# Loads placed behind the cast that frees their buffer, and every small transfer of attention and norms put on the sync queue

## The chip, the cores and the metric

The kernel runs on one core of a Trainium2 chip. A core has five engines that each work through their own list of instructions in order: PE (matrix products), DVE (vector), ACT (scalar), POOL (GpSimd) and SP (the sync engine, which here only issues DMA transfers). [...] The metric is the device time of one execution in microseconds (us), the median of several runs.

## The reference

A trunk of two layers on 256 tokens of width 2048, in float32. Each layer is a token mixer and an MLP, both behind an RMS norm and added into one residual stream:

```
for i in range(DEPTH):                                   # DEPTH = 2
    h = rms_norm(x, mix_norm_g[i])
    mix = fox_attention(...) if i % 2 == 0 else dilated_attention(...)
    x = x + mix
    h = rms_norm(x, mlp_norm_g[i])
    x = x + sq_relu_mlp(h, mlp_w_up[i], mlp_w_down[i])   # (relu(h @ up) ** 2) @ down
```

- `fox_attention`: 16 heads of 128. `h @ w_in` gives q, k, v and a forget gate per head; q and k are RMS-normed per head with a gain; the scores get the difference of cumulated log-sigmoid gates as a bias; causal softmax; `@ w_out`.
- `dilated_attention`: 8 heads with three groups of q and k each (dilations 1, 4, 16) and a shared v of 256; each group is a causal window of 128 strided steps with an ALiBi slope; the three groups are merged by their softmax denominators, which is one softmax over all of them; `@ w_out`.
- The MLP goes from 2048 to 8192 and back.

## The kernel before

**Weights.** All weights, some 420 MB, stream through the core once. `plan` (L207 to L257) lists pieces of 256 rows by 512 columns (512 KB), 800 of them, in the order of their use. `load()` (L280) puts one piece into one of five raw buffers (`RAW_BUFS`) by a transfer on the sync queue; in the dilated layer, where the columns of q and k lie apart, by two transfers of 256 KB. `split()` (L297) makes a high part `wh` in a reduced float format on ACT (L309, "the cast") and the rest `wl` by a subtraction on DVE (L310, "the cut"), each in five buffers (`W_BUFS`). A product is then three matmuls (L340 to L342): high by high, low by high, high by low; the MLP's first product (`transposed_steps`, L392) puts them into two (L404, L408). The matmuls of these weight products are called the main matmuls below. A raw buffer is free once cast and cut of its piece are done, and a pair of `wh` and `wl` once PE is through with its piece. `product_steps` (L330) calls `split()` after each piece, and `split()` calls `load()` first if its piece has not been asked for.

The fox layer's heads go in four groups of four: a weight product for q, one for k, one for v, and the heads' own work beside the next products.

**Side work.** Attention and norms run as Python generators under `Jobs` (L43). A `yield 4` means: go on four steps of the running weight product later; a step is one slice of 128 rows. `behind(x)` makes what is issued inside it stand behind the instruction `x` in its engine's list. Within these rules a planner in the framework, which works with its own estimates of durations, decides the final order of every engine's list when the program is built. The lists are fixed from then on; semaphores make an instruction wait for its inputs.

**Transposes through DRAM.** Several small matrices are transposed in 32 by 32 blocks on DVE, and the blocks are put into their places by writing them to DRAM and reading them back:

- `transposed_by_dma` (L431), for the norms: per token half four block writes (L440) and a read (L442), all on the sync queue, one behind the other.
- `qk_chain` (L513), for the heads' q and k: per token half four block writes on the sync queue (L544) and a read on POOL's queue (L545); the results are used 12 steps later.
- `p_turned` (L600), for softmax probabilities: four block writes (L610) one step after the transposition, and four steps later the read (L614), all on ACT's queue.

Also, `fox_head` (L730) loads each head's row of gate sums, spread over all partitions, on ACT's queue (`bias`, L742), and `gate_chain` writes them to DRAM on the sync queue (L727). `p_split` (L618) casts the turned probabilities (L623, L625) and `pv` (L584) multiplies them with v on PE (L593, L594, tiles `po_f` and `po_d`). `scores` (L653) computes a head's scores (tiles `sc_f`, `sc_d`; L657, L660); in the dilated layer DVE adds the ALiBi table (L799, tile `sd`). The last heads of a layer are transposed on PE instead (`p_transposed`, L628).

**The start.** Five pieces and x are loaded first; `more_constants` (L160) then loads the gate's weights `wf` (L164) and the gains, behind the load issued last at that point; `gate` (L667) multiplies with them (tile `pf`).

Of the kernel before, what the change touches and what calls it, by code (L numbers as in the profile page):

```python
# [89 lines left out]
def trunk(ctx: ExitStack, tc, x, fox_w_in, fox_b_f, fox_q_gain, fox_k_gain, fox_w_out, dil_w_in,  # L90
# [169 lines left out]
    def behind(*instructions):  # L260
        stack = ExitStack()
        for i in instructions:
            stack.enter_context(tc.issue_after(getattr(i, "ins", i)))
        return stack

    def hold(first):

        if "held" not in issued:
            return ExitStack()
        with behind(issued["gained"]):  # L270
            nc.vector.memset(first, 0.0)
        return behind(*([issued["load"]] if issued["held"] == [] else []))
# [24 lines left out]
    def split():  # L297
        i = state["split"]
        per = RAW_SUB // W_SUB
        if i >= len(plan) * per:  # L300
            return
        if i % per == 0 and state["raw"] <= i // per:
            load()
        raw = raws[i // per][:, (i % per) * W_SUB:(i % per + 1) * W_SUB, :]
        hi = wpool.tile([P, W_SUB, NC], F32R, tag="wh", name=f"wh{i}", bufs=W_BUFS)
        lo = wpool.tile([P, W_SUB, NC], F32R, tag="wl", name=f"wl{i}", bufs=W_BUFS)
        with behind(*([issued["gained"]] if i == 0 else issued.get("n0", []) if i < 2 * W_BUFS else [])):
            for part in ([slice(0, 1), slice(1, 2)] if i < 1 else [slice(0, W_SUB)]):
                issued["cast"] = nc.scalar.copy(hi[:, part, :], raw[:, part, :])  # L309
                issued["cut"] = nc.vector.tensor_sub(lo[:, part, :], raw[:, part, :], hi[:, part, :].bitcast(F32))  # L310
        splits.append((hi, lo))
        state["split"] += 1

# [114 lines left out]
    def transposed_by_dma(tag, col, n):  # L430


        tiles = []
        for t in range(NT):
            tile_ = work.tile([P, NC], F32, tag="w", name=f"turned_{tag}_{n}_{t}", bufs=5)
            blocks = dram.tile([4, 32, 4, P], F32, tag="blocks", name=f"blocks_{tag}_{n}_{t}", bufs=4)
            nc.vector.transpose(tile_.rearrange("p (j b r) -> p b j r", j=4, b=4),
                                xt[n][:, t, :].rearrange("p (b j c) -> p b j c", j=4, c=32))
            for i in range(4):
                nc.sync.dma_start(blocks[:, :, i, :].rearrange("j c x -> c j x"),  # L440
                                  tile_[32 * i:32 * i + 32].rearrange("p (j x) -> p j x", j=4))
            nc.sync.dma_start(tile_, blocks.rearrange("j c i x -> (j c) (i x)"))  # L442
            tiles.append(tile_)
        yield 9
        for half in range(2):
            pr = n * 2 + half
            both = act.tile([P, 2, 2, S], F32R, tag="hT", name=f"hT_{tag}_{pr}", bufs=KC // 2)
            for i in range(2):
                gc = gain[:, col + pr * 2 + i:col + pr * 2 + i + 1]
                for t in range(NT):  # L450
                    src = tiles[t].rearrange("p (i b r) -> p b i r", i=4, b=4)[:, half * 2 + i]
                    hi, lo = (both[:, i, x, t * P:(t + 1) * P].rearrange("p (i r) -> p i r", i=4) for x in range(2))
                    with behind(issued["cast"]):
                        on_act = nc.scalar.activation(hi, src, AF.Copy, scale=gc)
                    with behind(issued["cut"]):
                        on_dve = nc.vector.scalar_tensor_tensor(lo, src, gc, hi.bitcast(F32), ALU.mult, ALU.subtract)
            issued[tag, pr] = issued[tag] = on_act, on_dve
            hT[tag][pr] = both
            jobs.done.add((tag, pr))
            yield 1  # L460
# [52 lines left out]
    def qk_chain(acc, tag, key, parts):  # L513
# [21 lines left out]
            qn.append(q)  # L535


        for t in range(NT):
            turned = sq[t].rearrange("p (j h r) -> p j h r", j=4, h=4)
            nc.vector.transpose(turned.rearrange("p j h r -> p h j r"),  # L540
                                qn[t].rearrange("p h (j c) -> p h j c", c=32))
            blocks = dram.tile([4, 32, 4, P], F32, tag="blocks", name=f"blocks_{key}_{t}", bufs=4)
            for i in range(4):
                nc.sync.dma_start(blocks[:, :, i, :].rearrange("j c x -> c j x"), sq[t][32 * i:32 * i + 32].rearrange("p (j x) -> p j x", j=4))  # L544
            nc.gpsimd.dma_start(qn[t], blocks.rearrange("j c i x -> (j c) (i x)").rearrange("p (h d) -> p h d", h=4))  # L545
        yield 12
        for t in range(NT):
            yield 2
            for n, (c, nh, gcol, (whole, hi, lo)) in enumerate(parts):
# [50 lines left out]
    def p_turned(p, name):  # L600


        turned = work.tile([P, 4, 3, 32], F32, tag="s", name=f"turned_{name}", bufs=S_BUFS)
        nc.vector.transpose(turned.rearrange("p j b r -> p b j r"), p.rearrange("p (b j c) -> p b j c", b=3, c=32))
        yield 1

        blocks = dram.tile([4, 32, 4, 3 * 32], F32, tag="pblocks", name=f"pblocks_{name}", bufs=4)
        for i in range(4):
            with behind(issued["cast"]):
                nc.scalar.dma_start(blocks[:, :, i, :].rearrange("j c x -> c j x"),  # L610
                                    turned[32 * i:32 * i + 32].rearrange("p j b r -> p j (b r)"))
        yield 4
        with behind(issued["cast"]):
            nc.scalar.dma_start(turned.rearrange("p i b r -> p (i b r)"), blocks.rearrange("j c i x -> (j c) (i x)"))  # L614
        yield 4
        return turned

    def p_split(turned, name):  # L618
# [55 lines left out]
    def gate_chain(tag, pf):  # L674
# [49 lines left out]
        ct = work.tile([FH, 3 * P], F32, tag="s", name="g_ct", bufs=S_BUFS)  # L724
        nc.vector.tensor_scalar(ct[:, P:], pct, -1.0, None, ALU.mult)
        nc.vector.tensor_copy(ct[:, 0:P], ct[:, P:2 * P])
        nc.sync.dma_start(negc, ct)  # L727
        jobs.done.add("gate")

    def fox_head(j, hh, qT, kT, vt):  # L730
# [7 lines left out]
            yield at - 4  # L738

        bias = work.tile([P, 3 * P], F32, tag="bias", name=f"bias{h}", bufs=2)  # L740
        with behind(issued["cast"]):
            nc.scalar.dma_start(bias, negc[h:h + 1, :].to_broadcast([P, 3 * P]))  # L742
        yield 4
        nc.vector.tensor_add(bias, bias, tables["mask"])
        if hh == 0:
# [40 lines left out]
    def dil_head(q4, i, qTs, kTs, vt):  # L786
        h = 2 * q4 + i
        for g in range(3):
            yield ("dqk", q4, g)
        yield (3 if q4 == 3 else 6) * i + 1  # L790
        s = work.tile([P, 3, 3 * P], F32, tag="sd", name=f"sd{h}", bufs=1)
        for g in range(3):
            yield ("table", g)
            ps = ps_sc.tile([P, 512], F32, tag="sc", name=f"sc_d{h}_{g}")
            with behind(issued["product"]):
                for t in range(NT):
                    scores(ps, t, qTs[g], kTs[g], i)
            slope = 2.0 ** (-8.0 * (g * DH + h + 1) / N_SLOPES)
            nc.vector.scalar_tensor_tensor(s[:, g, :], tables[g], -slope, ps[:, 0:3 * P], ALU.mult, ALU.add)  # L799
            yield 1  # L800
        nm = small.tile([P, NT], F32, tag="nm", name=f"nm_d{h}")
        den = small.tile([P, NT], F32, tag="den", name=f"den_d{h}")
        spans = [slice(0, P), slice(P, 3 * P)]
        for t in range(NT):
            nc.vector.tensor_reduce(nm[:, t:t + 1], s[:, :, spans[t]], AX.XY, ALU.max, negate=True)
        yield 1
        for t in range(NT):
            nc.scalar.activation(s[:, :, spans[t]], s[:, :, spans[t]], AF.Exp, bias=nm[:, t:t + 1],
                                 accum_out=den[:, t:t + 1])
        yield 1  # L810
        nc.vector.reciprocal(den, den)
        p = work.tile([P, 3 * P], F32, tag="s", name=f"p_d{h}", bufs=S_BUFS)
        nc.vector.tensor_add(p, s[:, 0, :], s[:, 1, :])
        nc.vector.tensor_add(p, p, s[:, 2, :])
        for t in range(NT):
            nc.vector.tensor_scalar_mul(p[:, spans[t]], p[:, spans[t]], den[:, t:t + 1])
        if (q4, i) == (3, 1):
            yield 2
            pt_sb = p_transposed(p, f"d{h}")
        else:  # L820
            turned = yield from p_turned(p, f"d{h}")
            yield ("dv", q4)
            pt_sb = p_split(turned, f"d{h}")
        yield 3
        hi, lo = (act.tile([P, 2, S], F32R, tag=f"aT{x}", name=f"oTd{x}_{h}", bufs=KC // 2) for x in "hl")
        oT["d", h] = hi, lo
        yield from pv(pt_sb, vt, [i * S, i * S + P], [hi[:, 0, :], hi[:, 1, :]], [lo[:, 0, :], lo[:, 1, :]], f"d{h}")
        jobs.done.add(("od", h))
# [206 lines left out]
```

## Time and profile before

| | us |
|---|---|
| median of 3 runs (2158.12 to 2165.82) | 2159.53 |
| the profiled execution's own time | 2161.2 |
| its span, first to last instruction | 2159.5 |

| engine | busy us | share of the span |
|---|---|---|
| PE | 2142.0 | 99% |
| DVE | 1411.1 | 65% |
| ACT | 1098.5 | 51% |
| POOL | 66.0 | 3% |

The mean granted clock of PE is 0.998 of full speed. The sync queue carries 446 MB in transfers that take 65.9% of the 16 DMA engines' time, ACT's queue 12 MB (2.1%), POOL's 10.5 MB (1.5%). The fox layer's attention ends at about 330 us, the first MLP at about 1050, the dilated attention at about 1430, and the second MLP ends the run.

In the rows of the profile, `L309` is a line of the kernel, `wh<-raw` reads "tile wh, made from tile raw", and `ACTq` or `SPq` marks an instruction of that engine's queue that issues a transfer. A row of waits reads: engine, what waited, for whom; total us, times, longest. A row of the timeline reads: start, us, engine, line, operation, tiles, in brackets the idle time of the engine before it and what ended it. A row on one line's instructions gives durations in ns as least/median/greatest. In a list of transfers the last number is the median of us from issue to landing.

### The profile page before, as it was taken

To read this page: it belongs to the slowest core of one execution; us is meant where nothing else is said; L and a number is where in the kernel's file an instruction comes from. 1 tells how busy PE (TensorE), PEld (TensorE's weight loads), DVE (VectorE), ACT (ScalarE), POOL (GpSimd) and SP (SyncE) were. 2 spreads that over 40 slices of the span, in tenths; PEclk is the share of its full clock that TensorE was granted. 3 is DMA by queue.
4 is the path that set the end of the run, shared out by engine and by line. 5 is a ranking of instruction groups with operands and counts; after the bars stand their busy time and mean duration, and the time that the engine had idled before them with its cause. 6 is when DMAs were issued, how large, how long until landed. Compare 5 with 4: busy or idle time off the path is not lost.

```text
span 2159.5 us, 30045 instructions
## 1 busy us (share of the span) xinstructions
PE 2142.0 (99%) x11129; PEld 1905.7 (88%) x11129; DVE 1411.1 (65%) x1890; ACT 1098.5 (51%) x1524; POOL 66.0 (3%) x80
## 2 busy tenths in 40 slices
PE   9999999999999999999999999999999999999999
PEld 7888888998998998998888888888988988988988
DVE  6777778765665565566667777677655655655664
ACT  6564565644444454455555565646544543543442
POOL 0011000000000000000011010100000000000000
PEclk9999999999999999999999999999999999999999
DMA  7877777766766666667777776758666666666664
GB/s 251 254 251 216 231 254 244 250 202 204 202 202 202 203 201 202 202 203 242 242 233 231 239 237 209 262 185 282 205 204 202 199 204 204 199 203 204 201 211 145
DMA packets 309812, 470.79 MB, mean 218 GB/s; under 512 B 34649, under 2 KB 121889, under 8 KB 309665
## 3 DMA queue, kind: packets, MB, share of 16 engines
q1 hardware_dynamic: 288448, 446.30, 65.9%
q10 hardware_dynamic: 17984, 12.07, 2.1%
q0 software_dynamic: 3232, 10.50, 1.5%
q8 instruction: 87, 1.43, 0.3%
q14 instruction: 61, 0.49, 0.1%
HBM read 445.76 MB, written 23.03 MB: 217 GB/s over the span
## 4 chain that ended last, share of the span: by engine, by line
PE 91%; DMA 3%; DVE 2%; ACT 1%; issue 1%; SPq 0%; POOL 0%; ACTq 0%; DVEq 0%; POOLq 0%
PE acc L340 19%; PE acc L341 19%; PE acc L342 19%; PE up_n3a_acc L404 5%; PE up_n1a_acc L404 5%; PE up_n3a_sc L404 3%; PE up_n3a_tp L404 3%; PE up_n1a_tp L404 3%; PE up_n1a_sc L404 3%; PE up_n1a_acc L408 3%; PE up_n3a_acc L408 3%; PE up_n1a_sc L408 1%; PE up_n1a_tp L408 1%; PE up_n3a_tp L408 1%; PE up_n3a_sc L408 1%; DMA raw<-in_dil_w_in_dram 1%
## 5 line engine op out<-in xcount | busy, mean ns | idle before, releaser
L310 DVE TENSOR_TENSOR wl<-raw,wh 128x1024 fp32r<-128x1024 f32 (+1 forms) x801 | 974.4, 1220 | 645.2 <-ACT wh L309 643.3
L309 ACT CAST wh<-raw 128x1024 fp32r<-128x1024 f32 (+1 forms) x801 | 836.8, 1047 | 923.9 <-PE acc L342 503.0
L341 PE MATMUL acc<-wl,hT_n 128*128 128x512 f32 x896 | 341.5, 381 | 0.1
L340 PE MATMUL acc<-wh,hT_n 128*128 128x512 f32 x896 | 341.0, 383 | 0.2 <-ACT wh L309 0.2
L342 PE MATMUL acc<-wh,hT_n 128*128 128x512 f32 x896 | 341.1, 381 | 0.0
L340 PE MATMUL acc<-wh,aTh_n1a 128*128 128x512 f32 x512 | 194.0, 379 | 0.0
L341 PE MATMUL acc<-wl,aTh_n1a 128*128 128x512 f32 x512 | 194.0, 379 | 0.0
L342 PE MATMUL acc<-wh,aTl_n1a 128*128 128x512 f32 x512 | 194.0, 379 | 0.0
L340 PEld LDWEIGHTS acc<-wh,hT_n 128*128 128x128 f32 x896 | 170.2, 190 | 24.3 <-ACT wh L309 1.5
L342 PEld LDWEIGHTS acc<-wh,hT_n 128*128 128x128 f32 x896 | 170.3, 190 | 23.9
L341 PEld LDWEIGHTS acc<-wl,hT_n 128*128 128x128 f32 x896 | 170.4, 190 | 22.8 <-DVE wl L310 0.4
L340 PE MATMUL acc<-wh,aTh_n3a 128*128 128x512 f32 x480 | 181.9, 379 | 0.0
L341 PE MATMUL acc<-wl,aTh_n3a 128*128 128x512 f32 x480 | 181.9, 379 | 0.0
L342 PE MATMUL acc<-wh,aTl_n3a 128*128 128x512 f32 x480 | 181.9, 379 | 0.0
L404 PE MATMUL up_n1a_acc<-hT_n,wh 128*128 128x512 f32 x512 | 181.6, 382 | 0.0
L404 PE MATMUL up_n3a_acc<-hT_n,wh 128*128 128x512 f32 x512 | 181.6, 382 | 0.0
L408 PE MATMUL up_n3a_acc<-hT_n,wl 128*128 128x256 f32 x512 | 139.6, 273 | 0.0
L408 PE MATMUL up_n1a_acc<-hT_n,wl 128*128 128x256 f32 x512 | 139.6, 273 | 0.0
L341 PEld LDWEIGHTS acc<-wl,aTh_n1a 128*128 128x128 f32 x512 | 96.8, 189 | 13.7
L342 PEld LDWEIGHTS acc<-wh,aTl_n1a 128*128 128x128 f32 x512 | 96.8, 189 | 13.7
L340 PEld LDWEIGHTS acc<-wh,aTh_n1a 128*128 128x128 f32 x512 | 96.8, 189 | 13.7
L404 PEld LDWEIGHTS up_n1a_acc<-hT_n,wh 128*128 128x128 f32 x512 | 96.8, 189 | 13.5
(727 smaller groups left out, 3181.4 us busy)
## 6 DMA issues: line engine op xcount, KB each, us to landing
raw<-in_mlp_w_up_dram SPq DMA_DIRECT2D x256, 512.0 KB, 4.3
raw<-in_mlp_w_down_dram SPq DMA_DIRECT2D x256, 512.0 KB, 4.3
raw<-in_dil_w_in_dram SPq DMA_DIRECT2D x192, 256.0 KB, 4.3
raw<-in_fox_w_in_dram SPq DMA_DIRECT2D x95, 512.0 KB, 5.0
raw<-in_fox_w_out_dram SPq DMA_DIRECT2D x32, 512.0 KB, 4.9
raw<-in_dil_w_in_dram SPq DMA_DIRECT2D x32, 512.0 KB, 6.1
raw<-in_dil_w_out_dram SPq DMA_DIRECT2D x32, 512.0 KB, 4.9
blocks_n<-turned_n SPq DMA_DIRECT2D x96, 64.0 KB, 2.3
```

Of the source, the lines that this page charges most:

```text
L309: issued["cast"] = nc.scalar.copy(hi[:, part, :], raw[:, part, :])
L310: issued["cut"] = nc.vector.tensor_sub(lo[:, part, :], raw[:, part, :], hi[:, part, :].bitcast(F32))
L340: nc.tensor.matmul(acc[t], ah[:, tok], hi, start=first, stop=False)
L341: nc.tensor.matmul(acc[t], ah[:, tok], lo, start=False, stop=False)
L342: issued["product"] = nc.tensor.matmul(acc[t], al[:, tok], hi, start=False, stop=last)
L404: issued["product"] = nc.tensor.matmul(banks[b], hi[:, i, col], in_turn(tokens.rearrange("p x s -> p (x s)"), P // 2), start=first, stop=last)
L408: nc.tensor.matmul(banks[b][:, 0:S], lo[:, i, col], in_turn(tokens[:, 0, :], P // 2), start=False, stop=False)
```

## The change

- `split()` no longer loads its own piece. After its cast and cut it loads the piece that will take over the buffer just freed, the one four pieces past the next (`RAW_BUFS - 1`), if all loads up to it are out.
- A new helper `move(dst, src)` issues a transfer on the sync queue behind the load issued last. It takes over the norms' writes and reads (they were on the sync queue, without that rule), the writes and reads of q and k (reads were on POOL's queue), the writes and reads of the probabilities and the loads of `bias` (both were on ACT's queue, behind the last cast), and the write of the gate sums.
- The reads stand in a step of their own: for the norms three steps after the writes (then six until use, nine in all as before), for q and k four (then seven, 11 in all instead of 12), for the probabilities four as before, with the step ahead of the writes moved behind the read.
- In the dilated heads the first scores come one step later.

```
+    def move(dst, src):
+
+        with behind(issued["load"]):
+            return nc.sync.dma_start(dst, src)
...
     def split():
...
-        if i % per == 0 and state["raw"] <= i // per:
-            load()
...
         splits.append((hi, lo))
         state["split"] += 1
+        if state["raw"] == (i + 1) // per + RAW_BUFS - 1:
+            load()
...
     def transposed_by_dma(tag, col, n):
...
             for i in range(4):
-                nc.sync.dma_start(blocks[:, :, i, :].rearrange("j c x -> c j x"),
-                                  tile_[32 * i:32 * i + 32].rearrange("p (j x) -> p j x", j=4))
-            nc.sync.dma_start(tile_, blocks.rearrange("j c i x -> (j c) (i x)"))
-            tiles.append(tile_)
-        yield 9
+                move(blocks[:, :, i, :].rearrange("j c x -> c j x"),
+                     tile_[32 * i:32 * i + 32].rearrange("p (j x) -> p j x", j=4))
+            tiles.append((tile_, blocks))
+        yield 3
+        for tile_, blocks in tiles:
+            move(tile_, blocks.rearrange("j c i x -> (j c) (i x)"))
+        yield 6
...
     def qk_chain(acc, tag, key, parts):
...
             for i in range(4):
-                nc.sync.dma_start(blocks[:, :, i, :].rearrange("j c x -> c j x"), sq[t][32 * i:32 * i + 32].rearrange("p (j x) -> p j x", j=4))
-            nc.gpsimd.dma_start(qn[t], blocks.rearrange("j c i x -> (j c) (i x)").rearrange("p (h d) -> p h d", h=4))
-        yield 12
+                move(blocks[:, :, i, :].rearrange("j c x -> c j x"), sq[t][32 * i:32 * i + 32].rearrange("p (j x) -> p j x", j=4))
+            turns.append(blocks)
+        yield 4
+        for t in range(NT):
+            move(qn[t], turns[t].rearrange("j c i x -> (j c) (i x)").rearrange("p (h d) -> p h d", h=4))
+        yield 7
...
     def p_turned(p, name):
...
-        yield 1
-
         blocks = dram.tile([4, 32, 4, 3 * 32], F32, tag="pblocks", name=f"pblocks_{name}", bufs=4)
         for i in range(4):
-            with behind(issued["cast"]):
-                nc.scalar.dma_start(blocks[:, :, i, :].rearrange("j c x -> c j x"),
-                                    turned[32 * i:32 * i + 32].rearrange("p j b r -> p j (b r)"))
+            move(blocks[:, :, i, :].rearrange("j c x -> c j x"),
+                 turned[32 * i:32 * i + 32].rearrange("p j b r -> p j (b r)"))
         yield 4
-        with behind(issued["cast"]):
-            nc.scalar.dma_start(turned.rearrange("p i b r -> p (i b r)"), blocks.rearrange("j c i x -> (j c) (i x)"))
-        yield 4
+        move(turned.rearrange("p i b r -> p (i b r)"), blocks.rearrange("j c i x -> (j c) (i x)"))
+        yield 5
...
     def gate_chain(tag, pf):
...
-        nc.sync.dma_start(negc, ct)
+        move(negc, ct)
...
     def fox_head(j, hh, qT, kT, vt):
...
-        with behind(issued["cast"]):
-            nc.scalar.dma_start(bias, negc[h:h + 1, :].to_broadcast([P, 3 * P]))
+        move(bias, negc[h:h + 1, :].to_broadcast([P, 3 * P]))
...
     def dil_head(q4, i, qTs, kTs, vt):
...
-        yield (3 if q4 == 3 else 6) * i + 1
+        yield (3 if q4 == 3 else 6) * i + 2
```

More of the change, by code (lines that the diff above doesn't have):

```diff
@@ L450, in transposed_by_dma @@
                 for t in range(NT):
-                    src = tiles[t].rearrange("p (i b r) -> p b i r", i=4, b=4)[:, half * 2 + i]
+                    src = tiles[t][0].rearrange("p (i b r) -> p b i r", i=4, b=4)[:, half * 2 + i]
                     hi, lo = (both[:, i, x, t * P:(t + 1) * P].rearrange("p (i r) -> p i r", i=4) for x in range(2))
@@ L535, in qk_chain @@
             qn.append(q)
+        turns = []
         for t in range(NT):
```

## The prediction

> **What bounds the kernel now.** I read the first part of the page, then PE's waits, then windows of single stalls.
>
> ```profile
> PE 2142.0 (99%) x11129; PEld 1905.7 (88%) x11129; DVE 1411.1 (65%) x1890; ACT 1098.5 (51%) x1524; POOL 66.0 (3%) x80
> ```
>
> The span is 2159.5 us and PE is busy for 2142.0 of it. No edit here changes a matmul, so only the 17.5 us in which PE stands still, and what a stall does to its clock, can be won. Who PE waits for:
>
> ```profile
> PE po_f L593 <- ACT pTh_f L623: 4.8, 2, 3.4
> PE sc_d L657 <- DVE sd L799: 3.1, 3, 2.7
> PE spare L119 <- POOL ident masks.py:199: 2.5, 1, 2.5
> PE ps_g_mix L138 <- DMA g_mix<-in_mix_norm_g_dram: 2.0, 1, 2.0
> PE sc_f L660 <- ACT fkT_0h L561: 1.0, 1, 1.0
> PE acc L340 <- ACT wh L309: 0.2, 1, 0.2
> ```
>
> The rows of `spare` and `ps_g_mix` are the start, which nothing touches. Weights are waited for once, 0.2 us. What is left is attention: 4.8 us for two heads' turned probabilities (1.4 and 3.4), 3.1 and 1.0 us for scores. The longest wait has a sequel in the clock column (after the busy shares), the second longest, 2.7 us, has none:
>
> ```profile
> 198.60:205.50 6.90, 5.85 (x16) 4.93 (x17) 4.58 (x6) 5.17 (x9) 0.00 (x0) 0.51 0.71 236
> 1162.70:1170.00 7.30, 7.30 (x41) 6.58 (x42) 6.44 (x10) 3.64 (x6) 1.12 (x2) 1.00 0.82 250
> ```
>
> For 6.9 us after the 3.4 us wait PE runs at 0.51 of its clock: another 3.4 us lost. All that this change can reach is then 4.8 + 3.1 + 1.0 + 3.4 = 12.3 us, 0.57%.
>
> **The change part by part.** First, loads. In before they already wait for the same cut:
>
> ```profile
> SPq L288 <- DVE wl L310: 1132.9, 552, 5.5
> ```
>
> Counted in both built programs, with the small transfers left out, only loads 9 to 13 change place in the sync queue's order: the planner had put every other load behind its cut already. So this part is worth nothing outside the start. Its cover: a buffer is free at a cut and needed five pieces later, 5 x 12 matmuls x 0.216 = 13.0 us; a load lands 5.0 us after issue (row below), cast and cut take 1.05 and 1.22, so a load may be held about 5.7 us before PE sees it.
>
> ```profile
> 118.82 0.38 PE L341 MATMUL acc<-wl,hT_n 128*128 128x512 f32 x1
> 119.04 0.38 PE L342 MATMUL acc<-wh,hT_n 128*128 128x512 f32 x1
> L310 DVE TENSOR_TENSOR wl<-raw,wh 128x1024 fp32r<-128x1024 f32 (+1 forms) x801 | 974.4, 1220 | 645.2 <-ACT wh L309 643.3
> L309 ACT CAST wh<-raw 128x1024 fp32r<-128x1024 f32 (+1 forms) x801 | 836.8, 1047 | 923.9 <-PE acc L342 503.0
> raw<-in_fox_w_in_dram SPq DMA_DIRECT2D x95, 512.0 KB, 5.0
> ```
>
> Second, issues. ACT's queue loses 84 block writes, 21 reads and 16 bias loads, POOL's loses 40 reads of q and k; the sync queue gains all 161:
>
> ```profile
> L610 ACTq DMA_DIRECT2D pblocks_f<-turned_f x56: 309/448/1228, 94.6 to 313.4; - x56
> L614 ACTq DMA_DIRECT2D turned_f<-pblocks_f x14: 344/344/1820, 101.7 to 318.8; - x14
> L742 ACTq DMA_DIRECT2D bias<-negc x16: 326/333/445, 70.9 to 308.0; - x16
>   ACT wh L309: 5.7, 1
> ```
>
> 84 x 0.448 + 21 x 0.344 + 16 x 0.333 = 50 us leave ACT; with 40 x 0.344 = 14 us for POOL's reads (priced like ACT's), 64 us come to the sync queue over both attention layers. ACT is 51% busy and hides them, but its line is in order: a block write that waits for its transposition holds the casts behind it, once for 5.7 us (last row).
>
> Third, the two stalled heads. The fourth head of a group of heads, on ACT:
>
> ```profile
> 115.99 1.90 ACTq L610 DMA_DIRECT2D pblocks_f<-turned_f  x4
> 122.81 0.37 ACT L596 CAST oTfh<-po_f 128x256 fp32r<-128x256 f32 x1 [3.46 <-PE po_f L594]
> 123.03 0.34 ACTq L614 DMA_DIRECT2D turned_f<-pblocks_f  x1
> 128.76 0.40 ACT L623 CAST pTh_f<-turned_f 128x256 fp32r<-128x256 f32 x1 [1.62 <-DMA turned_f<-pblocks_f]
> 199.19 0.41 ACT L623 CAST pTh_f<-turned_f 128x256 fp32r<-128x256 f32 x1 [3.58 <-DMA turned_f<-pblocks_f]
> ```
>
> The writes were issued by 117.9; the read goes out at 123.03, behind a cast that stood 3.46 us waiting for PE. On the sync queue that cast is not ahead of it, though eight block writes of q and two loads are, so I count no earlier landing. What decides is PE's order: in the changed program this head's product stands 38 main matmuls later (head 3; 37 for head 7), 8.2 and 8.0 us, against waits of 1.4 and 3.4. Both go, and the half clock with the second: -8.2. Bounds: 0 if the heads' own chains come 8 us later, -8.2 at most. What is late next is the same head's input in the third group, which has no wait today.
>
> Fourth, heads put earlier on PE: head 0 by 14 matmuls (3.0 us), head 1 by 20 (4.3), the first dilated head by 23 (5.0). Their margin today:
>
> ```profile
> 106.48 0.40 ACT L623 CAST pTh_f<-turned_f 128x256 fp32r<-128x256 f32 x1
> 110.06 0.27 PE L593 MATMUL po_f<-pTh_f,fv0h 128*128 128x256 f32 x1
> 114.41 0.42 ACT L623 CAST pTh_f<-turned_f 128x256 fp32r<-128x256 f32 x1
> 119.47 0.27 PE L593 MATMUL po_f<-pTh_f,fv0h 128*128 128x256 f32 x1
> 1184.03 0.41 ACT L623 CAST pTh_d<-turned_d 128x256 fp32r<-128x256 f32 x1 [1.51 <-DVE ss_('dqk', 1, 1)_10876 L524]
> 1188.89 0.38 PE L593 MATMUL po_d<-pTh_d,dv0h 128*128 128x256 f32 x2
> ```
>
> 110.06 - 106.88 - 3.0 = 0.2 us; 119.47 - 114.83 - 4.3 = 0.3; 1188.89 - 1184.44 - 5.0 = -0.5. I take +0.5, at the near end since ACT is freed just there; the far end is priced in the first rival.
>
> Fifth, scores. The product of head 12 moves five matmuls (1.1 us) later against its 1.0 us wait: -1.0 (bounds -1.0 to 0). The dilated scores keep their place, and the loads that feed their chain stand behind a burst of eight block writes, to which two reads of 0.34 now come:
>
> ```profile
> 1139.15 1.80 SPq L544 DMA_DIRECT2D ks_('dqk', 0, 2)_0_10461<-sq_('dqk', 0, 2)_0_10386  x4
> 1141.05 1.85 SPq L544 DMA_DIRECT2D ks_('dqk', 0, 2)_1_10468<-sq_('dqk', 0, 2)_1_10388  x4
> 1143.30 6.60 SPq L288 DMA_DIRECT2D raw<-in_dil_w_in_dram  x10
> ```
>
> So +0.7. Bounds: -3.1, and +0.7 + 3.4 if 2.7 grows past the 3.4 that halved the clock.
>
> Sixth, the start. The gate's weights now stand behind load 13 instead of load 8, and the gate's product 16 matmuls (3.5 us) later on PE:
>
> ```profile
> 19.97 0.47 SPq L164 DMA_DIRECT2D wf<-in_fox_w_in_dram  x1
> DMA to landing us min/median/max: 7.6/7.6/7.6
> 29.14 0.71 SPq L288 DMA_DIRECT2D raw<-in_fox_w_in_dram  x1
> L671 PE MATMUL pf<-hT_n,wfs x32: 276/276/302, 34.6 to 38.2; 128*32 128x256 f32 x32
> ```
>
> 29.14 + 0.71 + 7.6 = 37.5 for landing, 38.3 with a cast and a subtraction of 0.4 each, against 34.6 + 3.5 = 38.1 on PE: +0.2, bounds 0 and +5 (7.6 is one sample).
> Last, heads 12, 13 and 15 now stand directly ahead of the output product that reads them, 20 matmuls later than head 12 does now. Result cast and subtraction take 0.37 + 0.42; six matmuls of other work cover most: +0.5, bounds 0 and +3.4. The norms' transfers stay on their queue; the mlp stretches that hide them show no wait of PE, and gain or lose nothing.
>
> **Sum.** -8.2 + 0.5 - 1.0 + 0.7 + 0.2 + 0.5 = -7.3. That is against this execution's span of 2159.5 (its own time was 2161.2, 1.7 outside the span). The median of the runs, 2159.53, is 1.7 below its time; taking 7.3 from the median gives 2152.2 us.
>
> **The rivals.**
> Reads late behind loads: slower. In one queue a turned read stands behind two loads issued just before it. If transfers move in strict turn, at the page's rate, it lands 2 x 0.512 / 218 GB/s = 4.8 us later.
>
> ```profile
> DMA packets 309812, 470.79 MB, mean 218 GB/s; under 512 B 34649, under 2 KB 121889, under 8 KB 309665
> turned_n<-blocks_n SPq DMA_DIRECT2D x24, 256.0 KB, 3.8
> turned_f<-pblocks_f ACTq DMA_DIRECT2D x14, 192.0 KB, 5.7
> ```
>
> It decides where the margin is under 4.8: head 0 waits 4.6, the first dilated head 5.3, each with 3.4 of half clock, 16.7 together; less the 8.2 (whose margins hold) and with the rest of the sum +0.4: 2159.5 + 8.9 = 2168; a third such wait, 4.6 + 3.4, gives 2176. Against it: reads of the norms, which are on the sync queue now, land after 3.8 us, less than the 5.7 of ACT's. [...] 0.15.
> Loads held by a read that waits: slower. A read waits for its block writes, and loads stand behind it. It decides past the 5.7 us of cover; three such holds of 3 us beyond it, each with 3.4 of half clock, cost 19: with the sum 2171. For it: 64 us more issue on one line; against: weights are waited for 0.2 us in the whole run. 0.10.
> All reachable idle goes: 2159.5 - 12.3 = 2147. For it, a freed ACT and DVE chain ahead of the scores; against, the dilated chain hangs on loads, not on ACT. 0.15.
> It does nothing that shows: loads stand where they stood, stalls change heads, 2159.5. For it, PE at 99%. 0.12.
>
> **How the numbers follow.** The forecast, 2152, has 0.48, with its own range 2149 to 2160. 0.5% is 10.8 us, about what a measurement can tell from no change; the forecast lies inside it. Faster by more: the third rival and an edge of the forecast, 0.16. Slower by more (past 2170.3): half of the first rival, the second, and a price I may have too low where several heads pass 3.4 us, 0.22. Within: 0.62. The range 2146 to 2171 leaves out a fifth.
>
> **What would show it.** Right: PE's wait for the turned probabilities under 1 us, no window at half clock after the start, block writes and reads with their waits gone from ACT's list, loads as late as before. Wrong: a wait of PE above 3 us at head 0 or the first dilated head with a half clock behind it, reads on the sync queue landing after 7 us or more, or PE waiting for cast weights.

## The result, and the profile after

The changed kernel takes 2165.41 us (median of 15 runs, 2162.95 to 2167.72), the kernel before 2161.93 in 15 runs beside it (2156.46 to 2165.82): a ratio of 1.0017, 95% interval 1.0009 to 1.0025, so 3.5 us more. A second comparison on another occasion gave 1.0024 (1.0013 to 1.0034). The forecast was 7.3 us less. The profiled execution has a span of 2163.5 us, 4.0 over the one shown of before. Its engines, and PE's waits:

```profile
PE 2145.4 (99%) x11129; PEld 1904.4 (88%) x11129; DVE 1409.8 (65%) x1890; ACT 1101.6 (51%) x1524; POOL 41.6 (2%) x40
```

```profile
PE spare L119 <- POOL ident masks.py:199: 2.5, 1, 2.5
PE sc_d L666 <- DVE sd L807: 2.3, 2, 2.0
PE ps_g_mix L138 <- DMA g_mix<-in_mix_norm_g_dram: 1.9, 1, 1.9
PE po_f L606 <- DVE s_f L765: 1.9, 1, 1.9
PE po_d L606 <- DVE pTl_d L634: 1.8, 1, 1.8
PE acc L348 <- DVE wl L313: 1.1, 2, 0.9
PE po_f L606 <- ACT pTh_f L632: 0.9, 1, 0.9
PE po_f L606 <- DVE pTl_f L634: 0.5, 2, 0.2
```

The two waits for turned probabilities that the forecast rested on (4.8 us) and the 1.0 us for scores are gone. Behind the start there are now eight kinds of wait (two of 0.2 us each are not shown), none over 2.1 us, and six of them name DVE. Where the time went shows in the first and last start of the first matmuls of each MLP (tiles `up_n1a` and `up_n3a`); before, and then after:

```profile
L404 PE MATMUL up_n1a_acc<-hT_n,wh x512: 382/382/382, 380.4 to 963.5; 128*128 128x512 f32 x171
L404 PE MATMUL up_n3a_acc<-hT_n,wh x512: 382/382/382, 1489.4 to 2072.5; 128*128 128x512 f32 x171
```

```profile
L411 PE MATMUL up_n1a_acc<-hT_n,wh x512: 382/382/382, 380.4 to 963.5; 128*128 128x512 f32 x171
L411 PE MATMUL up_n3a_acc<-hT_n,wh x512: 382/382/382, 1492.8 to 2076.0; 128*128 128x512 f32 x171
```

The first MLP starts at 380.4 in both: the fox layer, where 9.2 us of waits and half clock (4.8 + 1.0 + 3.4, by the forecast's reading) went, ends with nothing gained. (0.9 us of it was lost in the first 50 us, most of that to the half clock of the start, which ended at 12.5 us instead of 10.9: before it ended the starts of PE's matmuls of 512 columns were 0.43 us apart, and 0.22 afterwards.) The second MLP starts 3.4 us later, all of it lost in the dilated layer. Two things happened there. PE's wait for the first dilated scores fell from 2.7 to 2.0 us, but this time the clock halved behind it, and the first dilated head's turned probabilities were 1.8 us late. A window of the same length behind that wait, after (the clock is the number ahead of the DMA share):

```profile
1162.70:1166.10 3.40, 3.40 (x11) 2.77 (x10) 2.81 (x4) 0.00 (x0) 0.00 (x0) 0.51 0.64 170
```

and before, where the wait had been longer:

```profile
1162.70:1166.10 3.40, 3.40 (x19) 3.05 (x20) 3.26 (x5) 0.70 (x1) 0.58 (x1) 1.00 0.59 133
```

### The profile page after: what moved, and what is told of

It is laid out like the page before. It is cut to its first block, busy times and chain, and to the rows that moved or that the text cites. A ratio compares the mean times of both kernels' runs of the same rounds, so it can differ in the third digit from the quotient of the medians.

```text
span 2163.5 us, 29880 instructions
## 1 busy us (share of the span) xinstructions
PE 2145.4 (99%) x11129; PEld 1904.4 (88%) x11129; DVE 1409.8 (65%) x1890; ACT 1101.6 (51%) x1524; POOL 41.6 (2%) x40
## 4 chain that ended last, share of the span: by engine, by line
PE 89%; DVE 3%; issue 1%; ACT 0%; DMA 0%; POOL 0%; SPq 0%; ACTq 0%; DVEq 0%; POOLq 0%
PE acc L347 19%; PE acc L349 19%; PE acc L348 19%; PE up_n1a_acc L411 5%; PE up_n3a_acc L411 5%; PE up_n1a_sc L411 3%; PE up_n1a_tp L411 3%; PE up_n3a_sc L411 3%; PE up_n3a_tp L411 3%; PE up_n3a_acc L415 3%; PE up_n1a_acc L415 3%; DVE wl L313 1%; PE up_n3a_tp L415 1%; PE up_n3a_sc L415 1%; PE up_n1a_tp L415 1%; PE up_n1a_sc L415 1%
## 5 line engine op out<-in xcount | busy, mean ns | idle before, releaser
L411 PEld LDWEIGHTS up_n3a_acc<-hT_n,wh 128*128 128x128 f32 x512 | 96.8, 189 | 13.5
```

The costliest lines, as they stand in the source:

```text
L411: issued["product"] = nc.tensor.matmul(banks[b], hi[:, i, col], in_turn(tokens.rearrange("p x s -> p (x s)"), P // 2), start=first, stop=last)
```

## Experiments

The first theory, "order": the changed waiting steps put the heads at worse places on PE. Its rival, "queue": the small transfers on the sync queue cost the time, by what they do to the loads or by being late. Four kernels part the change into loads, queue and steps. In the tables, "fox" is the first start of `up_n1a`, "dilated" the time from there to the first start of `up_n3a` (it holds the first MLP, which is the same everywhere), each from one profiled execution. One stretch of 3.4 us at half clock more or less moves such a column by 1.7 us, so the ratios decide.

| kernel | median us | ratio to before | fox | dilated |
|---|---|---|---|---|
| before | | 1 | 380.4 | 1109.0 |
| after_again | 2165.80 | 1.0024 (1.0013 to 1.0034) | 380.6 | 1112.5 |
| loads_only | 2161.78 | 1.0003 (0.9993 to 1.0013) | 384.4 | 1108.8 |
| queue_only | 2167.31 | 1.0033 (1.0021 to 1.0046) | 383.5 | 1111.7 |
| steps_only | 2157.22 | 0.9986 (0.9977 to 0.9994) | 374.8 | 1114.7 |

**loads_only**, the kernel before with

```
-        if i % per == 0 and state["raw"] <= i // per:
-            load()
...
+        if state["raw"] == (i + 1) // per + RAW_BUFS - 1:
+            load()
```

> The kernel before with the new place of the loads alone (a load is issued behind the cut of the piece that frees its buffer); the small transfers stay on their queues and all waiting steps keep their length. If the loss comes from the small transfers or from the steps, this is the kernel before: ratio 0.9995 to 1.0005, PE waiting for the turned probabilities of heads 3 and 7 as before. If loads held behind cuts cost time (the gate's weights behind load 13, cast weights late), it already takes 1 to 3.5 us more than before, PE waits for wl or for wfs, and the ratio is 1.0005 to 1.0016.

The new place of the loads alone does nothing that can be measured. Its profile has the waits of heads 3 and 7 as before (1.2 and 3.5 us), and in this execution a third of 3.0 us at head 11 with a half clock behind it (mean clock 0.997, 0.998 in before), which is why its fox column is longer.

**queue_only**, the kernel after with the steps of before:

```
-        yield 7
+        yield 8
...
+        yield 1
         blocks = dram.tile([4, 32, 4, 3 * 32], ...)
...
-        yield 5
+        yield 4
         return turned
...
-        yield (3 if q4 == 3 else 6) * i + 2
+        yield (3 if q4 == 3 else 6) * i + 1
```

> The kernel after, with the loads behind cuts and all small transfers on the sync queue, but with the waiting steps of before (1, 4 and 4 in the turn of probabilities, 4 and 8 behind the writes of q and k, 1 ahead of a dilated head). Theory 'order': what costs is the place on PE that the changed steps give the heads; then this one is at or under before (ratio 0.997 to 1.000), and the waits of 0.9 at head 1, 1.9 at head 9 and 1.8 at the first dilated head are gone. Theory 'queue': what costs is the small transfers standing in line with the loads; then this one is where after is, 3 to 5 us over before (ratio 1.0014 to 1.0023).

**steps_only**, the kernel before with the steps of after (the same lines the other way round; 12 becomes 11).

> The kernel before, every transfer on its old queue and the loads in their old place, with the waiting steps of after (0, 4 and 5; 11 in place of 12; 2 in place of 1 ahead of a dilated head). Theory 'order': 3 to 5 us over before (ratio 1.0014 to 1.0023), with new waits of PE at heads 1 and 9 and at the first dilated head. Theory 'queue': before or a little under it (ratio 0.997 to 1.000), heads 3 and 7 without their waits of 1.4 and 3.4 us.

**after_again**, the kernel after beside them.

> The kernel after itself, beside the three others on the same chip: ratio 1.0009 to 1.0025. If a half clock of some 3.4 us that comes in some executions and not in others is what parts the two kernels, the executions whose mean clock is 1.000 should agree: both near a span of 2156. If after has more small waits, its executions at clock 1.000 have a span near 2161, 5 us over the lowest of before.

"Order" as a matter of the steps falls: the steps alone win 0.14%, and the queue with the loads' place costs 0.33%, at least as much as all of after and more than was expected of it. In its profiled execution, the slowest of its eleven, steps_only does in the fox layer what the forecast wanted (374.8 against 380.4) and loses all of it in the dilated one, to a wait of PE of 5.6 us (in a total of 6.0) and 6.8 us at half clock:

```profile
PE sc_d L655 <- DVE sd L797: 6.0, 3, 5.6
...
PE sc_f L658 <- ACT fkT_0h L561: 2.1, 3, 1.0
```

After_again also bears out what was expected of the clock: its one execution at a mean clock of 1.000 had a span of 2160.8, and before's at 1.000 had 2155.7. So after is some 5 us slower with the half clock left out of both.

The next four ask which transfers it is. Theory "probabilities" against "any small transfer in the loads' line":

| kernel | median us | ratio to before | fox | dilated |
|---|---|---|---|---|
| p_back | 2160.24 | 0.9987 (0.9977 to 0.9997) | 377.0 | 1110.0 |
| q_back | 2158.87 | 0.9988 (0.9979 to 0.9997) | 376.4 | 1108.6 |
| p_only | 2176.58 | 1.0066 (1.0053 to 1.0078) | 393.8 | 1110.4 |
| later_scores | 2155.38 | 0.9967 (0.9955 to 0.9979) | 373.9 | 1110.8 |

**p_back**, the kernel after with

```
-            move(blocks[:, :, i, :].rearrange(...), turned[...])
+            with behind(issued["cast"]):
+                nc.scalar.dma_start(blocks[:, :, i, :].rearrange(...), turned[...])
...
-        move(turned.rearrange(...), blocks.rearrange(...))
+        with behind(issued["cast"]):
+            nc.scalar.dma_start(turned.rearrange(...), blocks.rearrange(...))
```

> The kernel after with the probabilities' block writes and reads alone put back on ACT's queue behind the last cast; loads, reads of q and k, bias and norms stay on the sync queue, all steps as in after. Theory 'probabilities': it is these transfers whose move to the sync queue makes the planner put the heads' products up to 31 main matmuls elsewhere on PE, and the short waits at pTh, pTl and at the cut follow from that; then this one is where steps_only is, ratio 0.997 to 1.0005, and the waits for pTh_f and pTl_f are under 0.5 us together. Theory 'any small transfer in the loads' line': each kind costs its part, 64 of the 161 issues are still there, and this one is half way, ratio 1.0003 to 1.0015.

**q_back**, the kernel after with

```
-            turns.append(blocks)
-        yield 4
-        for t in range(NT):
-            move(qn[t], turns[t].rearrange(...))
-        yield 7
+            nc.gpsimd.dma_start(qn[t], blocks.rearrange(...))
+        yield 11
```

> The kernel after with the reads of q and k alone put back on POOL's queue right behind their writes (11 steps ahead of use in one piece). Theory 'probabilities': as slow as after, ratio 1.0009 to 1.003. Theory 'any small transfer in the loads' line': 40 reads of 256 KB are the largest part by bytes, so this one is well under after, ratio 0.999 to 1.0005.

**p_only**, steps_only with the two `move` lines of p_back's diff put in, and nothing else.

> steps_only (the steps of after, all else as before) with the probabilities' block writes and reads alone moved to the sync queue behind the load issued last. In the built program the heads' products then stand 11 to 31 main matmuls (2.4 to 6.7 us) earlier on PE than in steps_only. Theory 'probabilities': PE waits for turned probabilities at most of the 21 heads, 1 to 3 us each, 5 to 20 us in all over steps_only (ratio to before 1.001 to 1.008). Theory 'any small transfer in the loads' line': a part of after's loss, 1 to 3 us over steps_only (ratio 0.999 to 1.0003). If the chip delivers them earlier as planned, no loss at all.

Either part put back undoes the whole loss, so neither theory holds as it was put: "probabilities" falls at q_back, "any small transfer" at p_back, which should have been half way. In after the loss takes both. But the parts do not add up: p_only moves the probabilities alone and is much slower than after, in the amount "probabilities" expected and mostly not by its mechanism. PE waits 8.2 us for cast weights and 1.4 for turned probabilities, and in the fox layer it runs for 10.2 us at half clock (the mean clock is 0.997):

```profile
PE acc L344 <- ACT wh L313: 8.2, 3, 3.1
...
PE po_f L597 <- DVE pTl_f L625: 1.0, 3, 0.5
...
PE po_f L597 <- ACT pTh_f L623: 0.4, 1, 0.4
```

The sync queue's issues of p_only show why for the first of the three waits for weights (the last row is ACT's cast that waited for the load):

```profile
101.58 0.68 SPq L292 DMA_DIRECT2D raw<-in_fox_w_in_dram  x1
...
105.99 7.49 SPq L268 DMA_DIRECT2D pblocks_f<-turned_f  x5
113.65 0.34 SPq L268 DMA_DIRECT2D turned_f<-pblocks_f  x1
114.04 0.91 SPq L268 DMA_DIRECT2D pblocks_f<-turned_f  x2
115.87 1.76 SPq L548 DMA_DIRECT2D blocks_('fq', 1)_0_1248<-sq_('fq', 1)_0_1179  x4
117.74 1.85 SPq L548 DMA_DIRECT2D blocks_('fq', 1)_1_1255<-sq_('fq', 1)_1_1181  x4
119.63 0.98 SPq L292 DMA_DIRECT2D raw<-in_fox_w_in_dram  x2
...
124.41 1.04 ACT L313 CAST wh<-raw 128x1024 fp32r<-128x1024 f32 x1 [8.80 <-DMA raw<-in_fox_w_in_dram]
```

The queue's list is in order: block writes that wait for DVE hold the loads behind them, and no load goes out from 102.3 to 119.63. That is the forecast's second rival (loads held), in a kernel that has the transfers but not the new place of the loads. In steps_only the probabilities' writes are on ACT's queue, and no load stands behind them; p_loads, below, prices the loads' place at about 6 us.

**later_scores**, steps_only with the dilated heads' first scores later in the first group:

```
-        yield (3 if q4 == 3 else 6) * i + 1
+        yield (3 if q4 == 3 else 6) * i + (5 if q4 == 0 else 2)
```

(against before, beside the other steps).

> The kernel before with its queues and loads, the steps of after in the turn of probabilities and of q and k, and the first group of dilated heads' scores 18 main matmuls (3.9 us) later on PE than in steps_only, where PE waited 5.6 us for them and lost 2.9 us at half clock behind it. If that wait is set by DVE's list and not by PE's place, it stays, and the time with it (2157). If the later place takes it, 1.7 us of wait are left and no half clock: a span near 2153, ratio to before 0.995 to 0.998.

The later place took 3.4 of the 5.6 us, and no half clock came. 2.2 us are left where 1.7 were expected, and 1.6 us for the first dilated head's probabilities are new.

**A new theory.** In the kernel after, what PE waits for at 250 and 1186 us (and at 206 and 1160) stands on DVE's list behind an instruction that stands still. DVE at 1184 to 1188, where PE waits 1.84 us for `pTl_d`:

```profile
1184.16 0.20 DVE L533 TENSOR_SCALAR ss_('dqk', 1, 1)_10893<-ss_('dqk', 1, 1)_10893 128x8 f32<-128x8 f32 x1
...
1186.59 0.36 DVE L539 TENSOR_SCALAR rq_('dqk', 1, 1)_10897<-rq_('dqk', 1, 1)_10897,rstd_n 128x4 f32<-128x4 f32 x2 [1.50 <-POOL rq_('dqk', 1, 1)_10897 L535]
1186.86 0.69 DVE L541 TENSOR_TENSOR qn_('dqk', 1, 1)_0_10937<-acc,rq_('dqk', 1, 1)_10897 128x512 f32<-128x512 f32 x1
1187.46 0.41 DVE L634 TENSOR_TENSOR pTl_d<-turned_d,pTh_d 128x256 fp32r<-128x256 f32 x1
```

POOL raises eight numbers per partition to a power, and DVE stands 1.50 us for them with the small subtraction queued behind. The turned probabilities were there 2.6 us before: ACT began their cast at 1184.82. In q_back the same subtraction stands ahead of the stand, and PE waits 0.2 us:

```profile
1178.61 0.23 DVE L533 TENSOR_SCALAR ss_('dqk', 1, 1)_10893<-ss_('dqk', 1, 1)_10893 128x8 f32<-128x8 f32 x1
1178.68 0.49 DVE L631 TENSOR_TENSOR pTl_d<-turned_d,pTh_d 128x256 fp32r<-128x256 f32 x1
...
1181.41 0.36 DVE L539 TENSOR_SCALAR rq_('dqk', 1, 1)_10897<-rq_('dqk', 1, 1)_10897,rstd_n 128x4 f32<-128x4 f32 x2 [1.56 <-POOL rq_('dqk', 1, 1)_10897 L535]
```

The wait at 250 us is the same thing with one more link (it is at head 8, the first of the third group; the expectations of queue_only and steps_only call it head 9). DVE stands 1.75 us for POOL, then reads head 10's scores, and only that frees the score bank in which head 8's product is to be put:

```profile
249.12 0.36 DVE L539 TENSOR_SCALAR rq_('fq', 3)_2589<-rq_('fq', 3)_2589,rstd_n 128x4 f32<-128x4 f32 x2 [1.75 <-POOL rq_('fq', 3)_2589 L535]
...
251.59 0.74 DVE L765 SCALAR_TENSOR_TENSOR s_f<-sc_f,c_q,bias 128x128 f32<-128x128 f32 x2
...
252.47 0.35 PE L606 MATMUL po_f<-pTh_f,fv2h 128*128 128x256 f32 x1 [1.86 <-DVE s_f L765]
```

The test is one rule, which lets DVE come to `rq` a little later in its list:

```
+            with behind(issued["cut"]):
-            nc.vector.tensor_scalar_mul(rq[:, t, :], rq[:, t, :], rstd[tag][:, t:t + 1])
+                nc.vector.tensor_scalar_mul(rq[:, t, :], rq[:, t, :], rstd[tag][:, t:t + 1])
```

| kernel | median us | ratio to before | fox | dilated |
|---|---|---|---|---|
| after_rq | 2160.21 | 0.9992 (0.9982 to 1.0001) | 378.2 | 1110.4 |
| before_rq | 2158.63 | 0.9985 (0.9975 to 0.9995) | 380.2 | 1106.8 |
| later_scores_rq | 2150.63 | 0.9947 (0.9935 to 0.9960) | 372.0 | 1107.1 |
| p_loads | 2170.76 | 1.0040 (1.0026 to 1.0053) | 390.0 | 1111.3 |

**after_rq**, the kernel after with this rule.

> The kernel after with one rule added: DVE's product of rq (the per-head factors of q and k that POOL raises to a power) stands behind the cut issued last, so that DVE comes to it later in its list; the sync queue's order is the same, line for line. Theory 'DVE stands for POOL': in after DVE stands 1.5 to 1.8 us for POOL at 205, 249, 1154 and 1185 us, and PE's waits of 0.9, 1.9, 2.0 and 1.8 us right behind follow from that; with the rule they are under 0.7 each, 4 to 7 us go and the ratio to before is 0.998 to 1.000. Theory 'sync queue': what PE waits for comes late off the sync queue; then the waits stay within 0.5 us of after's and the ratio is 1.001 to 1.0025.

**before_rq**, the kernel before with it.

> The kernel before with the same rule for rq; PE's order is the same but for one instruction. If DVE's stand for POOL is a cost of both kernels, this one is 2 to 4 us under before (the 2.7 us wait of the dilated scores is shorter): ratio 0.998 to 0.9993. If it only hurts in after's order, ratio 0.9993 to 1.0007.

**later_scores_rq**, later_scores with it.

> later_scores with the same rule for rq. PE's waits there are 2.2 us for the first dilated scores and 1.6 us for the first dilated head's turned probabilities, both behind DVE's stand for POOL. If that is their cause, 2 to 4 us go: a median of 2151 to 2153.5, ratio to before 0.9945 to 0.9965. If not, 0.9965 to 0.998 as later_scores.

After_rq issues on the sync queue line for line as after does, its reads of the fox layer's probabilities land after 5.4 us (5.5 in after), and it is no slower than before: most of the loss came from the order of the engines' lists, and not from late transfers. The rule moves some 70 of DVE's instructions in after, and with them some 30 of PE's and 6 of ACT's, so DVE's part is not separated from theirs here. In before it moves 27 of DVE's, one of PE's and none of ACT's, and wins 0.15%: there the gain is DVE's. DVE's stand is a cost of both kernels, and after's order put more of PE's inputs behind it. With the rule in both, after_rq is still 1.6 us above before_rq, at the edge of the noise.

The wait at 250 is down to 0.1 us, the cut's at 206 is gone, that for the dilated scores is 0.5. Head 1's wait of 0.9 us stays; behind it is no stand of DVE for POOL. A cut at 147 us and the second group's probabilities at 184 are waited for anew, 0.6 and 1.0 us. The wait of 1.8 at the first dilated head is only down to 1.4, since DVE still stands there, for 1.1 us; those parts of the expectation missed. Later_scores_rq beats both kernels, 0.53% under before, and behind the start this is what is left of PE's waits in it:

```profile
PE po_d L594 <- ACT pTh_d L622: 0.9, 1, 0.9
PE sc_d L656 <- DVE sd L798: 0.2, 1, 0.2
PE acc L340 <- ACT wh L309: 0.2, 1, 0.2
```

**p_loads**, p_only with the diff of loads_only.

> p_only with the new place of the loads added (a load behind the cut of the piece that frees its buffer). In p_only two loads of the first group went out 18 and 19 us after their buffer was free, behind eight block writes of probabilities and eight of q that each wait for DVE, and PE waited 8.2 us in three places for the casts of such loads. Theory 'loads held': with the loads asked for ahead of those writes the waits for the casts go and 8 to 15 us with them: ratio to before 0.999 to 1.003. Theory 'order of the heads': the products still stand up to 38 main matmuls earlier than in after, so PE's waits only change their name, ratio 1.004 to 1.008.

The loads' new place takes the waits for casts away and about 6 us with them (2176.58 to 2170.76, ratios 1.0066 and 1.0040), less than expected. The rest stays under other names, as "order of the heads" had it:

```profile
PE po_f L599 <- DVE pTl_f L627: 5.2, 3, 2.4
PE po_f L599 <- ACT pTh_f L625: 4.7, 2, 2.5
PE sc_d L659 <- DVE sd L801: 4.0, 3, 3.1
```

So the part of the change that does nothing alone is needed by the part that puts the probabilities on the loads' queue. Counted in the built programs, the place of four heads' products on PE, in main matmuls against before:

```
head   steps_only   p_only   p_loads   q_back   after
  0        +15        -14       -14       -14     -14
  1         -6        -31       -31       -20     -20
  3         +5        -12       +36       +38     +38
  8        +17        -14        -2        -7      +6
```

With the probabilities off ACT's list the planner, by its own estimates, puts products earlier (p_only). Each further part of the change puts some of them later again: the loads' place head 3 (p_loads), the bias loads and the writes of q and k, of the norms and of the gate sums head 1 (q_back), the reads of q and k head 8 (after). In after the transfers changed their queue, but most of what changed the time is the order that the planner then wrote for PE, ACT and DVE. Why it chooses each place was not tried, and no kernel moves the transfers and keeps the lists of before.

## Why the prediction was wrong

The forecast of 7.3 us less came out as 3.5 us more. The gains that it counted came; what it did not price was the new order of the other engines' lists.

**What bounds the kernel, and the stalled heads (-8.2): right.** PE's waits of 1.4 and 3.4 us at heads 3 and 7 are gone (0.2 us is left at head 7), with the half clock. Measured by matmul starts, 1.57 + 3.54 + 2.97 = 8.1 us came back. The half clock had begun 1.0 us before the wait ended, so it cost 2.97 us and not the 3.4 of the forecast. The 1.0 us for head 12's scores went too.

**Fourth step, heads put earlier (+0.5): this is the step that failed.** It took three margins (0.2, 0.3 and -0.5 us) from before, as if the heads' inputs came at the old time. Head 0 indeed does not wait; head 1 waits 0.9 us, the first dilated head 0.2 + 1.8 = 2.0, so 2.9 in place of 0.5. In neither case does a row show ACT or DVE waiting for the read; the cast or the subtraction of the probabilities stood on ACT or DVE behind other work that waited. For the first dilated head the rows are those above, of DVE at 1184 to 1188; for head 1 it is ACT, which waits for DVE's maxima of another head's scores:

```profile
116.39 0.40 ACT L771 ACTIVATE s_f<-s_f,nm_f 128x128 f32<-128x128 f32 x1 [0.83 <-DVE nm_f L768]
...
117.28 0.39 ACT L632 CAST pTh_f<-turned_f 128x256 fp32r<-128x256 f32 x1
```

I compared places on PE and on the sync queue. Some 240 of DVE's 1890 instructions stand elsewhere in its list than in before, and I priced none of them.

**A term was missing: DVE's new order at the other heads.** The wait at head 8 (1.9), two cuts (0.9 and 0.2), heads 7 and 11 (0.2 each) and the fox scores (0.4 together) come to 3.8 us. Beside them, some 18 more matmul starts of the fox layer than in before come over 0.03 us late without a wait, about 2 us together; why stays open. Each wait also costs some 0.17 us more than its row shows, start to start (1.57 for 1.40, 3.54 for 3.37), and there are 11 in the fox layer where there were 4.

**Fifth step, dilated scores (+0.7): the wait was mis-sized, and its price was wrong in kind.** The wait fell by 0.7; the half clock that I had tied to waits past 3.4 us came behind one of 2.0, and took 1.7. How the two waits lay in time is in the last section; the forecast did not look at it.

**Loads (0): right, and too narrow.** Alone they are worth nothing (1.0003). I did not see that the probabilities' move needs them (p_only, p_loads). They do come earlier: ACT's waits for loads fall, which never reached PE. Before:

```profile
ACT wh L309 <- DMA raw<-in_dil_w_in_dram: 19.4, 7, 4.3
ACT wh L309 <- DMA raw<-in_fox_w_in_dram: 16.1, 9, 3.6
ACT wh L309 <- DMA raw<-in_fox_w_out_dram: 13.0, 2, 8.1
```

After:

```profile
ACT wh L312 <- DMA raw<-in_fox_w_in_dram: 10.9, 11, 3.0
ACT wh L312 <- DMA raw<-in_dil_w_in_dram: 3.2, 4, 2.2
ACT wh L312 <- DMA raw<-in_fox_w_out_dram: 2.3, 2, 1.5
```

"Loads as late as before", one of the signs named as right, was a miss. So was "no window at half clock after the start", and "under 1 us" for the probabilities holds for each wait of the fox layer, not for the dilated one of 1.8. None of the signs named as wrong came (the latest read whose landing is on record took 6.6 us).

**Start (+0.2) and the last heads (+0.5):** 0.14 us each, the second less than priced. The 0.6 us that the half clock of the start took more had no term.

**The rivals.** Reads late behind loads: not what happened. Beside the loads the norms' reads land later than before, the fox layer's probabilities no later, and PE's waits do not end with a landing. After:

```profile
turned_n<-blocks_n SPq DMA_DIRECT2D x24, 256.0 KB, 5.4
turned_f<-pblocks_f SPq DMA_DIRECT2D x14, 192.0 KB, 5.5
```

Before had 3.8 and 5.7. The 4.8 us later of this rival was an estimate that no run shows, and the landings do not go by the queue alone: with the probabilities on ACT's queue their reads land after 2.7 us in steps_only and 5.7 in before, and the dilated layer's after 2.3 in before on ACT's queue and 2.4 in after on the sync queue. Loads held: it is real in p_only, and no wait of PE in after shows it. "Stalls change heads" (0.12) is nearest to what happened, with the dilated layer's 3.4 us on top.

## What to carry to other kernels

Where a planner writes the lists, moving a transfer to another queue changes the order of engines that the transfer does not touch. Compare every engine's list, and look for what stands behind an instruction that waits for a slow engine, before pricing the move by landings. Transfers that wait for compute do not belong ahead of loads on an in-order queue, unless the loads are asked for early enough to stand ahead of them: PE waited 8.2 us for cast weights in p_only, and p_loads, with the loads ahead, took about 6 us less in all.

## What the hardware showed that was not expected

**The half clock did not go by the length of the wait alone.** In before it came behind the wait of 3.4 us, for 6.8 us, and not behind the one of 2.7; in after behind 2.0 us, for 3.4, and not behind 1.9 (at 250) or 1.8 (at 1186); in steps_only behind 5.6 us, for 6.8; and not behind 2.2 us in later_scores (a clock of 1.00 from 1159.0 to 1162.4). In after_rq it came behind one of 1.4 us:

```profile
1180.60:1182.10 1.50, 0.06 (x2) 0.04 (x1) 1.38 (x5) 0.00 (x0) 0.09 (x1) 1.00 0.95 302
1182.40:1185.80 3.40, 3.40 (x14) 3.04 (x13) 3.26 (x6) 1.79 (x3) 0.00 (x0) 0.50 0.72 230
```

In the two traces of before and after these stretches lie on steps of 3.413 us, counted from the time at which full clock was first granted (in before 10.91 us, and 55 steps later 198.65; in after 12.46, and 337 steps later 1162.76; the half clock at the end of after, at 2162.86, is 630 steps behind that 12.46). In the step ahead of before's stretch PE stood still for 2.4 us, in the one ahead of after's for 2.0, waits and smaller gaps together; in any other step of the two, ahead of the last 10 us, it was 1.4 us at most, and no stretch began behind it. Before's wait of 2.7 us fell on two steps, after's of 2.0 on one. PE's busy time, the second number, in before's two steps:

```profile
1157.79:1161.20 3.41, 2.09 (x11) 1.50 (x9) 3.41 (x7) 1.04 (x1) 0.00 (x0) 1.00 0.61 196
1161.20:1164.62 3.42, 2.00 (x12) 1.87 (x13) 3.38 (x6) 0.00 (x0) 0.58 (x1) 1.00 0.55 138
```

and in after's:

```profile
1159.34:1162.75 3.41, 1.36 (x9) 0.96 (x8) 3.41 (x6) 1.01 (x1) 0.00 (x0) 1.00 0.59 167
```

That the idle time of a step decides is an estimate of mine from these two executions; no run tested it, and in after_rq the wait that took a half clock was no longer than before's of 1.4 us at 128, behind which the clock stayed full. Full clock came at 10.91 us in one execution and at 12.46 in the other, so by this estimate the same wait can be punished in one and not in the next. That fits the spread: the same program before ran with spans of 2155.7 us at a mean clock of 1.000 and of 2166.7 at 0.997.

**A power of eight numbers per partition is slow on POOL.** POOL takes 1.6 to 2.7 us for one in before and after, and DVE stood for it 20 times in before and 19 times in after, up to 1.9 us; letting it do other work meanwhile gave 0.15% in before (before_rq) and about 0.3% in after (1.0017 or 1.0024 to 0.9992, with the moves on PE and ACT).
